# First stage of a hybrid encoder layer: modulation and projection by quarters of K, with four row tiles together

## The chip, the core and the metric

The kernel runs on one core of a Trainium2 chip. The metric is the device time of one execution in microseconds, as the median of several runs. TensorE is called PE here, VectorE DVE, ScalarE ACT, GpSimd POOL and SyncE SP; SP issues the loads and stores of this stage.

## The reference

The input x has 2048 rows of 1024 values (D = 1024), c is one conditioning vector of 1024 values. The reference is one encoder layer; what matters here is its beginning:

```python
mod = silu(c) @ w_mod + b_mod                      # w_mod: 1024 x 6144
shift1, scale1, gate1, shift2, scale2, gate2 = split(mod, 6)
hmix = rms_norm(x, g_norm1) * (1.0 + scale1) + shift1
proj = hmix @ w_in                                 # w_in: 1024 x IN_COLS
q_a, k_a, v_a, q_m, k_m, v_m, o_m, gates = split(proj, ...)
...                                                # windowed attention and a two-way mLSTM,
x = x + gate1 * (concat(att, h_m) @ w_out)         # then the output projection
hff = rms_norm(x, g_norm2) * (1.0 + scale2) + shift2
gte, up = split(hff @ w_ffn_in, 2)
x = x + gate2 * ((silu(gte) * up) @ w_ffn_out)
out = rms_norm(x, g_final)
```

All of it is float32. The modulation is six rows of 1024 values, numbered m = 0 to 5 in the order of the split: m = 1 (scale1) and m = 0 (shift1) are needed before anything can be projected, m = 2 (gate1) and m = 3 to 5 later.

## The kernel before

A product of float32 matrices is made of three products of rounded halves (`mm3`, L56 to L58: high by high, high by low, low by high), so every operand is split into a high part (a rounded copy) and a low part (the difference).

**The first stage** makes, for 16 row tiles of 128 rows (four blocks of four tiles), the "natural" projection: rows on partitions, and 656 columns of w_in: 128 of v_a, 16 of gates and 128 of the first v_m head in one bank (`pa`, 272 columns), the other 384 of v_m in a second one (`pv`). K is 1024, in eight slices k of 128. Its steps:

- *Modulation.* Rows m = 1 and m = 0 are made in halves z of 512 columns. `load_mod` reads a half as four tiles `wmod` of 128 x 2 x 512. `mod_sum` multiplies the slices by the columns of silu(c) (`sc_col`) on DVE and sums them (`macc`, L213 and L215). For two of the four sums, PE takes the first four slices as row products; the row goes through ACT to columns. For the others, four column products with a vector of ones (`modps`, L230) sum over the partitions. `mod_bias` (L237) adds the bias, and `scales` (L328) makes the factor `gs` = (1 + scale) x g.
- *Norm.* For a block of 512 rows: ACT squares and sums (L168), DVE takes the reciprocal root in small steps (`rsqrt`, L106 among them), then the rows are scaled in place (L175 on ACT or L177 on DVE).
- *Transposes.* `turned_split` turns one slice k of a block: PE transposes four 128 x 128 pieces into a bank (`trn`, L183), ACT applies factor and shift (`ntmp`, L184), DVE writes the high part and the low part (`hT`, L190 and L191).
- *Weights.* `load_nat` and `split_nat` load a half of w_in's 656 columns (`wnr`) and split it: ACT writes `wnh` (L346), DVE and POOL share the differences `wnl` (L347).
- *Products.* `nat_mm` (L397) makes the products of one tile over a list of slices k: all k for `pa`, then all k for `pv`.
- *Evictions.* For each tile, ACT writes `vs` from `pa` (L478), DVE its low part and the gates, ACT two pieces of `va`; SP stores `vs` and `va` (L486, L487). `vs` has one buffer.
- *The gate row.* `mod_row(2)` (L359) is drawn, step by step, behind tiles 4, 5 and 6: loads of `wmod` into the buffers big24 to big27, eight sum steps on DVE (`macc`, L375), a split (L141), and two products on PE (`modrow`, L381).

The order on PE is written out by hand (`hand`). On the other engines it is by hand up to `pre.close()` (L439), and a planner orders them behind that. The buffers are reused: x of block 1 lies in big24 to big27, and the weights of modulation in big8 to big15.

Before, tiles 0, 1 and 2 go through k = 0 to 3 when the first half of the modulation is there, and through k = 4 to 7 when the second is. Tile 3 follows in one piece. `EVERY` says behind how many steps of `nat_mm` one slice of the next block is turned; its first row, (0, 0, 0, 2), puts the eight slices of block 1 into tile 3, its second row, eights, two slices of block 2 into each of tiles 4 to 7.

Behind the first stage come the projections in columns, attention, mLSTM, output projection and FFN.

Of the kernel before, what the change touches and what calls it, by code (L numbers as in the profile page):

```python
# [11 lines left out]
F32 = mybir.dt.float32  # L12
# [3 lines left out]
AF = mybir.ActivationFunctionType  # L16
# [20 lines left out]
def hybrid_layer_kernel(  # L37
# [148 lines left out]
    def turned_split(pl, xt, k, gs, shift, dst):  # L186
# [3 lines left out]
        dve.tensor_copy(dst(0, k), t)  # L190
        dve.tensor_tensor(dst(1, k), t, dst(0, k).bitcast(F32), SUB)  # L191

    wm_slots = deque(range(8, 16))

    def load_mod(m, z):

        r = []
        for k in range(0, KT, 2):
            w = big(wm_slots[0], "wmod", (P, 2, 512), F32)
            wm_slots.rotate(-1)  # L200
            sp.dma_start(w, w_mod[k * P:(k + 2) * P, m * D + z * 512:m * D + (z + 1) * 512]
                         .rearrange("(k p) c -> p k c", p=P))
            r.append(w)
        return r

    def mod_sum(pl, m, z, ws_, n_pe):


        acc = pl.tile([P, 512], F32, tag="macc", name="macc")
        for k in range(n_pe, KT):  # L210
            w = ws_[k // 2][:, k % 2, :]
            if k == n_pe:
                dve.tensor_scalar(acc, w, sc_col[:, k:k + 1], None, MUL)  # L213
            else:
                dve.scalar_tensor_tensor(acc, w, sc_col[:, k:k + 1], acc, MUL, ADD)  # L215
        yield True
        if n_pe:
            ps = bank("b", "modrow")
            for k in range(n_pe):
                pe.matmul(ps[:1, :], sc_col[:, k:k + 1], ws_[k // 2][:, k % 2, :], start=k == 0, stop=False)  # L220
            pe.matmul(ps[:1, :], ones[:, 0:1], acc, start=False, stop=True)
            row = pl.tile([1, 512], F32, tag="mrow", name="mrow", bufs=1)
            act.activation(row, ps[:1, :], AF.Copy)
            ps = bank("b", "modps")
            for k in range(4):
                pe.matmul(ps[:, k:k + 1], row[:, k * P:(k + 1) * P], ones[:1, 0:1], start=True, stop=True)
        else:
            ps = bank("d", "modps")
            for k in range(4):
                pe.matmul(ps[:, k:k + 1], acc[:, k * P:(k + 1) * P], ones[:, 0:1], start=True, stop=True)  # L230
        yield True
        mod_bias(m, z, ps)
        yield True

    def mod_bias(m, z, ps):
        o = O_BM + m * KT + 4 * z
        dve.tensor_tensor(mod[:, m, 4 * z:4 * z + 4], ps[:, :4], cols[:, o:o + 4], ADD)  # L237

    wslots = deque()

# [37 lines left out]
    with tc.tile_pool(name="sw", bufs=2, side="right", reuse_waits="tile") as sw:  # L278
# [16 lines left out]
            return r  # L295

        xts = [load_x(0)]
        wm = {(m, 0): load_mod(m, 0) for m in (1, 0)}
# [26 lines left out]
        BD = (slice(0, 4), slice(4, 8))  # L325

        def scales(z):
            dve.scalar_tensor_tensor(gs1[:, BD[z]], mod[:, 1, BD[z]], 1.0, cols[:, O_G1 + 4 * z:O_G1 + 4 * z + 4], ADD, MUL)  # L328

        def load_nat(z):  # L330

            w4 = w_in[z * 512:(z + 1) * 512].rearrange("(k p) c -> p k c", p=P)
            r = [big(16 + 4 * z, "wnr", (P, 4, 144), F32)] + [big(17 + 4 * z + i, "wnr", (P, 2, 512), F32) for i in range(2)]
            sp.dma_start(r[0][:, :, 0:128], w4[:, :, C_VA:C_VA + 128])
            sp.dma_start(r[0][:, :, 128:144], w4[:, :, C_G:C_G + 16])
            for i in range(2):
                sp.dma_start(r[1 + i], w4[:, 2 * i:2 * i + 2, C_VM:C_VM + 512])
            return r

        def split_nat(z, r):  # L340
            ks = BD[z]
            act.activation(wh[:, ks, :144], r[0], AF.Copy)
            dve.tensor_tensor(wl[:, ks, :144], r[0], wh[:, ks, :144].bitcast(F32), SUB)
            for i in range(4):
                k, v = 4 * z + i, r[1 + i // 2][:, i % 2]
                act.activation(wh[:, k, 144:], v, AF.Copy)  # L346
                (pool, dve)[i % 2].tensor_tensor(wl[:, k, 144:], v, wh[:, k, 144:].bitcast(F32), SUB)  # L347

        def norm1(n, xt):
            hT.append(Kt(n, f"hT{n}"))  # L350
# [46 lines left out]
        def nat_mm(n, i, pa, pv, ks):  # L397
            for o, cs in ((pa[:, :NA], slice(0, NA)), (pv[:, :NV], slice(NA, NA + NV))):
                for k in ks:
                    lh, ll = (hT[n](s, k, slice(i * P, (i + 1) * P)) for s in (0, 1))  # L400
                    mm3(o, lh, ll, wh[:, k, cs], wl[:, k, cs], k == 0, k == KT - 1)
                    yield True

        wn = [load_nat(0)]
        wm[1, 1] = load_mod(1, 1)
        wn.append(load_nat(1))
        wm[0, 1] = load_mod(0, 1)
        xts += [load_x(1), load_x(2)]
        for src, o, n in ((g_norm2, O_G2, 8), (conv_b, O_CB, 8), (conv_w[0], O_CW, 24), (g_attn_out, O_GA, 4), (g_mlstm_out, O_GM, 4)):
            sp.dma_start(rows[1][o - N_A:o - N_A + n, :], src.rearrange("o (a b) -> (o a) b", b=P))  # L410
        hT.append(Kt(0, "hT0"))
        ms = {(m, z): mod_sum(s1, m, z, wm[m, z], 4 if m == 1 - z else 0) for z in range(2) for m in (1, 0)}
        ssq = squares(s1, xts[0])
        r = rsqrt(s1, ssq, 4, D, "rs")
        next(ms[1, 0])
        scaled(xts[0], r, True)
        next(ms[0, 0])
        next(ms[1, 0])
        next(ms[1, 0])
        next(ms[0, 0])  # L420
        next(ms[0, 0])
        scales(0)
        split_nat(0, wn[0])
        ops = {i: (bank("gga"[i], "pa"), bank("acc"[i], "pv")) for i in range(3)}
        for k in range(4):
            turned_split(s1, xts[0], k, gs1, mod[:, 0, :], hT[0])
        for i in range(3):
            deque(nat_mm(0, i, *ops[i], range(4)), 0)
        next(ms[1, 1])
        split_nat(1, wn[1])  # L430
        next(ms[1, 1])
        next(ms[1, 1])
        next(ms[0, 1])
        next(ms[0, 1])
        next(ms[0, 1])
        scales(1)
        for k in range(4, KT):
            turned_split(s1, xts[0], k, gs1, mod[:, 0, :], hT[0])
        pre.close()  # L439
        gn = cp.tile([P, 2, 2, HM, NT], F32, name="gn")  # L440
        bgv = bg.rearrange("p (d y h) -> p y d h", d=2, y=2)
        vecs = iter(())
        EVERY = ((0, 0, 0, 2), (8, 8, 8, 8), (2, 0, 0, 0), (0, 0, 0, 0))
        for n in range(NB):
            if n + 1 < NB:
                nrm = norm1(n + 1, xts[n + 1])
                next(nrm)
            if n == 0:
                xts.append(load_x(3))
            if n == 1:  # L450
# [6 lines left out]
                w_first = proj_cols(C_KM)  # L457
            for i in range(4):
                tt = 4 * n + i
                if tt < 3:  # L460
                    pa, pv = ops[i]
                else:
                    pa, pv = bank("g", "pa"), bank("a", "pv")
                ev = EVERY[n][i]
                for j, _ in enumerate(nat_mm(n, i, pa, pv, range(4 if tt < 3 else 0, KT))):
                    if ev and j % ev == ev - 1:
                        next(nrm, None)
# [9 lines left out]
                pav = pa[:, :128].rearrange("p (k d) -> p k d", k=KV)  # L477
                act.activation(vs[:, :, 0, :], pav, AF.Copy)  # L478
                dve.tensor_tensor(vs[:, :, 1, :], pav, vs[:, :, 0, :].bitcast(F32), SUB)
                dve.tensor_tensor(gn[:, :, :, :, tt], pa[:, 128:144].rearrange("p (d y h) -> p y d h", d=2, y=2), bgv, ADD)  # L480
                act.activation(va[:, 0, :128], pa[:, 144:272], AF.Copy)
                act.activation(va[:, 1:, :128], pv[:, :384].rearrange("p (h d) -> p h d", d=128), AF.Copy)
                pool.memset(va[:, :, 128:129], 1.0)
                if tt != 9:
                    next(vecs, None)
                sp.dma_start(vst_d[tt * P:(tt + 1) * P], vs.bitcast(F32))  # L486
                sp.dma_start(vaug_d[tt * P:(tt + 1) * P], va)  # L487
# [1464 lines left out]
```

## Time and profile before

| | |
|---|---|
| runs | 2285.49, 2286.15, 2283.78 us; median 2285.49 |
| span of the profiled execution | 2283.0 us |
| instructions | 32,447 |
| PE busy | 2224.0 us, 97% |
| DVE busy | 1610.1 us, 71% |
| ACT busy | 1058.6 us, 46% |
| POOL busy | 1069.3 us, 47% |
| DMA | 391.28 MB, mean 171 GB/s |

How to read it: the span goes from the first to the last instruction of one profiled execution. The profiled execution's own time is this span, with what lies around it not in the trace; the median of the runs is 2.5 us above it. A row of a trace's timeline has start and duration in us, the engine, the line of the kernel (L), the operation, what it writes and reads, and in brackets the wait ahead of it and what ended it. A row of the groups has busy time in us, mean ns of one, and behind the bar the idle time of the engine just ahead of these instructions with what ended most of it. A row of the windows has the stretch and its length, then the busy us and the instructions (x) of PE, PEld (weight loads), DVE, ACT and POOL, then the granted clock of PE (1.00 is full speed), the busy share of the DMA engines, and GB/s.

### The profile page before, as it was taken

How to read it: one execution, taken by the hardware profiler on the slowest of the kernel's cores; microseconds unless marked ns; L12 is line 12 of the kernel's file. 1: busy time of each engine (PE TensorE's matmuls, PEld its weight loads, DVE VectorE, ACT ScalarE, POOL GpSimd, SP SyncE). 2: the span in 40 equal slices, each digit the busy share in tenths (PEclk: the TensorE clock that was granted, in tenths of full speed). 3: DMA queues.
4: the chain of work that ended last, by engine and by line, in shares of the span. 5: the costliest groups of instructions: out<-in, count | busy, mean ns of one | idle time of the engine just before them, and what ended most of it. 6: DMA issues, size and time to landing. Idle time of an engine off the chain costs nothing.

```text
span 2283.0 us, 32447 instructions
## 1 busy us (share of the span) xinstructions
PE 2224.0 (97%) x10822; PEld 1859.5 (81%) x10822; DVE 1610.1 (71%) x2931; ACT 1058.6 (46%) x2206; POOL 1069.3 (47%) x927
## 2 busy tenths in 40 slices
PE   6999999999999999999999999999999999999998
PEld 4997788888788878788888888788888888888887
DVE  6787577656687887786756776666766666785594
ACT  5433565644577755344444444433333333233352
POOL 1006535334333434536656665566666654592020
PEclk9999999999999999999999999999999999999999
DMA  8476755676666576764353453533333374542462
GB/s 331 157 242 213 238 152 172 186 229 191 194 179 186 177 234 218 267 221 134 111 171 111 152 180 134 178 108 108 100 106 103 105 255 147 162 155 93 140 220 92
DMA packets 352811, 391.28 MB, mean 171 GB/s; under 512 B 21260, under 2 KB 251004, under 8 KB 352644
## 3 DMA queue, kind: packets, MB, share of 16 engines
q1 hardware_dynamic: 352420, 389.18, 52.5%
q8 instruction: 85, 1.39, 0.2%
q14 instruction: 82, 0.67, 0.1%
q10 hardware_dynamic: 224, 0.04, 0.0%
HBM read 269.95 MB, written 119.19 MB: 170 GB/s over the span
## 4 chain that ended last, share of the span: by engine, by line
PE 51%; DVE 3%; DMA 1%; issue 1%; ACT 1%; POOL 1%; SPq 0%; ACTq 0%; POOLq 0%; DVEq 0%
PE fp L56 11%; PE fp L57 11%; PE fp L58 11%; PE fo L58 5%; PE fo L57 5%; PE fo L56 5%; PE ops L56 1%; PE ops L57 1%; DMA al<-a_d 1%; PE ops L58 1%; DVE w L1721 1%; DVE al L1712 1%; DVE ra L1851 1%; PE trn L183 0%; DMA T<-hop_d 0%
## 5 line engine op out<-in xcount | busy, mean ns | idle before, releaser
L498 PE MATMUL gps<-hT,whi 128*128 128x512 f32 x1088 | 397.3, 420 | 0.3 <-DVE cacc L513 0.3
L57 PE MATMUL fo<-w,ah 128*128 128x512 f32 x616 | 239.8, 389 | 1.1 <-DVE w L1721 1.1
L58 PE MATMUL fo<-w,al 128*128 128x512 f32 x616 | 239.8, 389 | 0.5 <-DVE al L1712 0.5
L56 PE MATMUL fo<-w,ah 128*128 128x512 f32 x616 | 239.7, 389 | 0.0
L498 PE MATMUL gps<-hT,wlo 128*128 128x512 f32 x544 | 226.9, 417 | 0.0
L498 PEld LDWEIGHTS gps<-hT,whi 128*128 128x128 f32 x1088 | 200.5, 191 | 24.5 <-DVE cacc L513 0.7
L56 PE MATMUL fp<-T,S 128*128 128x512 f32 x528 | 206.9, 392 | 1.9 <-ACT s L1608 1.9
L57 PE MATMUL fp<-T,S 128*128 128x512 f32 x528 | 205.6, 389 | 0.0
L58 PE MATMUL fp<-T,S 128*128 128x512 f32 x528 | 205.4, 389 | 0.0
L1712 DVE TENSOR_TENSOR al<-al,ah 128x1024 fp32r<-128x1024 f32 x77 | 119.3, 1552 | 109.2 <-ACT ah L1711 109.0
L1711 ACT ACTIVATE ah<-al 128x1024 fp32r<-128x1024 f32 x77 | 81.6, 1060 | 188.5 <-DMA al<-a_d 186.9
L1451 DVE TENSOR_TENSOR S<-sf,S 128x512 fp32r<-128x512 f32 x86 | 130.4, 1554 | 37.4 <-ACT S L1450 37.2
L1451 DVE TENSOR_TENSOR A<-graw,A 128x512 fp32r<-128x512 f32 x86 | 128.4, 1515 | 16.3 <-ACT A L1450 16.3
L58 PE MATMUL fp<-B,A 128*128 128x512 f32 x352 | 136.9, 389 | 0.0
L56 PE MATMUL fp<-B,A 128*128 128x512 f32 x352 | 136.9, 389 | 0.0
L57 PE MATMUL fp<-B,A 128*128 128x512 f32 x352 | 136.9, 389 | 0.0
L57 PEld LDWEIGHTS fo<-w,ah 128*128 128x128 f32 x616 | 115.6, 188 | 25.6 <-DVE w L1721 1.6
L58 PEld LDWEIGHTS fo<-w,al 128*128 128x128 f32 x616 | 115.6, 188 | 24.9 <-DVE al L1712 1.0
L56 PEld LDWEIGHTS fo<-w,ah 128*128 128x128 f32 x616 | 115.6, 188 | 24.3 <-ACT ah L1711 0.2
L1616 DVE SCALAR_TENSOR_TENSOR g<-t,g 128x512 f32<-128x512 f32 x44 | 41.3, 939 | 132.2 <-ACT t L1615 132.2
L1455 POOL TENSOR_TENSOR sf<-A,A22r 128x512 f32<-128x512 f32 x43 | 61.0, 1419 | 154.9 <-DMA A22r<-in_w_ffn_in_dram 130.8
L798 POOL TENSOR_SCALAR ap<-ap,adn 128x384 f32<-128x384 f32 (+1 forms) x128 | 73.0, 590 | 129.2 <-DVE adn L796 71.7
(418 smaller groups left out, 6166.8 us busy)
## 6 DMA issues: line engine op xcount, KB each, us to landing
al<-a_d SPq DMA_DIRECT2D x77, 512.0 KB, 3.8
wmod<-in_w_mod_dram SPq DMA_DIRECT2D x48, 512.0 KB, 7.3
graw<-in_w_ffn_in_dram SPq DMA_DIRECT2D x43, 512.0 KB, 4.0
a_d<-ka SPq DMA_DIRECT2D x66, 256.0 KB, 4.6
bc<-bc_d SPq DMA_DIRECT2D x64, 256.0 KB, 3.7
hop_d<-n SPq DMA_DIRECT2D x56, 256.0 KB, 4.5
a_d<-u SPq DMA_DIRECT2D x55, 256.0 KB, 4.8
mqk<-qk_d SPq DMA_DIRECT2D x44, 256.0 KB, 4.0
```

The source lines that it names most:

```text
L56: pe.matmul(o, lh, rh, start=first, stop=False, skip_group_check=skip)
L57: pe.matmul(o, lh, rl, start=False, stop=False, skip_group_check=skip)
L58: pe.matmul(o, ll, rh, start=False, stop=last, skip_group_check=skip)
L498: pe.matmul(ps, w[i == 2][:, k, :], hT[n](i == 1, k), start=(k == 0 and i == 0), stop=(k == KT - 1 and i == 2))
L798: pool.tensor_scalar(self.p[g][:, :self.NK], self.p[g][:, :self.NK], dn[:, g:g + 1], 0.0, MUL, ADD)
L1451: dve.tensor_tensor(t[:, 1, :], f, t[:, 0, :].bitcast(F32), SUB)
L1455: pool.tensor_tensor(f1, a21, a22, ADD)
L1616: dve.scalar_tensor_tensor(g0, t0, 1.0, g0, ADD, MUL)
L1711: act.activation(ah, al.bitcast(F32), AF.Copy)
L1712: dve.tensor_tensor(al, al.bitcast(F32), ah.bitcast(F32), SUB)
L1721: dve.tensor_tensor(w[:, 1, :], f, w[:, 0, :].bitcast(F32), SUB)
L1851: dve.tensor_tensor(ra[i], ra[i], xr, ADD)
```

## The change

K now goes by quarters q of 256, that is two slices k, and all four tiles of block 0 go through K together.

- *Modulation* (class `Mod`). A quarter of a row m is 256 columns, read as two tiles of 128 x 4 x 256. DVE sums slices in steps of 256 columns. Column products leave the result as columns at once (`product`, two for each slice or sum): in the first quarter PE takes the slices k = 0, 1, 2, 4 and 6 itself, in the other three DVE sums all eight and PE only closes the sum. `close` adds the bias and, for m = 1, makes the quarter of `gs`.
- *Weights* come by quarters: `nat_hi` on ACT, and `nat_lo` wholly on DVE.
- *Transposes of block 0.* `turned_hi`: ACT reads the bank twice, and writes the high part and `ntmp`; DVE only subtracts.
- *Products.* `few_mm(i, k)` makes the products of tile i with one slice k. Four tiles have six banks: two of tag g, shared by two tiles each, and four of tags a and c; an odd tile has 240 columns in the shared bank and 416 in its own. `outs` says where the evictions find the columns.
- *Order.* The main loop over q places loads, sums, transposes and products. Loads of x for blocks 1 and 2 stand in the third quarter. Behind `pre.close()`, tile 0's turn makes the last products of k = 6 and 7 for tiles 0 and 1, tiles 2 and 3 follow; tiles 4 and 5 then run as a pair, two slices k at a time, with the slices of block 1 turned just ahead of them (`nrm1`). `EVERY` becomes ((0,0,0,0), (0,0,4,4), ...): block 2's slices go into tiles 6 and 7.

Behind tile 8 the instructions of every engine stand in the same order in both kernels. The diff, cut to its core:

```diff
+    def turned_hi(pl, ps, k, gs, shift, dst):
+        act.activation(dst(0, k), ps, AF.Identity, bias=shift[:, k:k + 1], scale=gs[:, k:k + 1])
+        t = pl.tile([P, 512], F32, tag="ntmp", name="ntmp", bufs=2)
+        act.activation(t, ps, AF.Identity, bias=shift[:, k:k + 1], scale=gs[:, k:k + 1])
+        dve.tensor_tensor(dst(1, k), t, dst(0, k).bitcast(F32), SUB)
...
-    def load_mod(m, z):
...
-    def mod_sum(pl, m, z, ws_, n_pe):
...
+    class Mod:
+        def __init__(self, m, q, on_pe):
...
+                w = big(wm_slots[0], "wmod", (P, 4, 256), F32)
+                wm_slots.rotate(-1)
+                sp.dma_start(w, w_mod[k * P:(k + 4) * P, m * D + q * 256:m * D + (q + 1) * 256]
+                             .rearrange("(k p) c -> p k c", p=P))
+        def part(self, pl, h):
+            for k in range(4 * h, 4 * h + 4):
+                w = self.w[h][:, k % 4, :]
+                if k in self.on_pe:
+                    continue
+                if self.acc is None:
+                    self.acc = pl.tile([P, 256], F32, tag="macc", name="macc", bufs=3)
+                    dve.tensor_scalar(self.acc, w, sc_col[:, k:k + 1], None, MUL)
+                else:
+                    dve.scalar_tensor_tensor(self.acc, w, sc_col[:, k:k + 1], self.acc, MUL, ADD)
+        def product(self, w, col, tag, last=False):
+            for j in range(2):
...
+                pe.matmul(self.ps[:, j:j + 1], w[:, j * P:(j + 1) * P], col, start=first, stop=last, skip_group_check=True)
...
+        def close(self, tag):
+            self.product(self.acc, ones[:, 0:1], tag, True)
+            m, o = self.m, O_BM + self.m * KT + 2 * self.q
+            qs = slice(2 * self.q, 2 * self.q + 2)
+            dve.tensor_tensor(mod[:, m, qs], self.ps[:, :2], cols[:, o:o + 2], ADD)
+            if m:
+                dve.scalar_tensor_tensor(gs1[:, qs], mod[:, 1, qs], 1.0, cols[:, O_G1 + 2 * self.q:O_G1 + 2 * self.q + 2], ADD, MUL)
...
+        def load_quarter(q):
+            wm[1, q] = Mod(1, q, () if q else (0, 1, 2, 4, 6))
+            wn[q] = load_nat(q)
+            wm[0, q] = Mod(0, q, () if q else (0, 1, 2, 4, 6))
...
-        def split_nat(z, r):
...
-                (pool, dve)[i % 2].tensor_tensor(wl[:, k, 144:], v, wh[:, k, 144:].bitcast(F32), SUB)
+        def nat_lo(q, i):
+            k, r = 2 * q + i, wn[q]
+            dve.tensor_tensor(wl[:, k, 144:], r[1][:, i], wh[:, k, 144:].bitcast(F32), SUB)
...
+        def few_mm(i, k):
+            two = ((spare[i // 2][:, 272 * (i % 2):(512 if i % 2 else 272)], slice(0, (272, 240)[i % 2])),
+                   (ops[i][:, :(384, 416)[i % 2]], slice((272, 240)[i % 2], NA + NV)))
...
+        for q in range(4):
+            if q < 2:
+                load_quarter(q + 2)
+            if q == 2:
+                xts.append(load_x(1))
...
+                xts.append(load_x(2))
+            k = 2 * q
+            turned_hi(s1, trn[k], k, gs1, mod[:, 0, :], hT[0])
+            nat_hi(q, 1)
+            nat_lo(q, 1)
+            turned_hi(s1, trn[k + 1], k + 1, gs1, mod[:, 0, :], hT[0])
+            if q == 3:
+                break
+            for i in range(4):
+                few_mm(i, k)
+            wm[1, q + 1].part(s1, 0)
+            wm[1, q + 1].part(s1, 1)
+            wm[1, q + 1].close("b")
+            nat_hi(q + 1, 0)
+            nat_lo(q + 1, 0)
+            for i in range(2):
+                few_mm(i, k + 1)
+            trn[k + 2] = turns(xts[0], k + 2, "b")
+            wm[0, q + 1].part(s1, 0)
+            wm[0, q + 1].part(s1, 1)
+            wm[0, q + 1].close("d")
+            for i in range(2, 4):
+                few_mm(i, k + 1)
+            trn[k + 3] = turns(xts[0], k + 3, "d")
         pre.close()
...
-        EVERY = ((0, 0, 0, 2), (8, 8, 8, 8), (2, 0, 0, 0), (0, 0, 0, 0))
+        EVERY = ((0, 0, 0, 0), (0, 0, 4, 4), (2, 0, 0, 0), (0, 0, 0, 0))
...
+                if tt < 4:
+                    for j in (((6, 0), (6, 1), (7, 0), (7, 1)), (), ((6, 2), (7, 2)), ((6, 3), (7, 3)))[i]:
+                        few_mm(j[1], j[0])
+                    pg, vm = outs(i)
+                elif tt == 4:
+                    two = [(bank("g", "pa"), bank("a", "pv")) for _ in range(2)]
+                    next(nrm1)
+                    for k in range(0, KT, 2):
+                        for j in range(2):
+                            next(nrm1, None)
+                            deque(nat_mm(n, j, *two[j], (k, k + 1)), 0)
...
```

More of the change, by code (lines that the diff above doesn't have):

```diff
@@ L191, in turned_split @@
         dve.tensor_tensor(dst(1, k), t, dst(0, k).bitcast(F32), SUB)
-    wm_slots = deque(range(8, 16))
-    def load_mod(m, z):
[L197 to L204, printed above, removed]
-    def mod_sum(pl, m, z, ws_, n_pe):
[L209 to L233, printed above, removed]
@@ L416, in hybrid_layer_kernel @@
[L416 to L430, printed above, removed]
@@ L431, in hybrid_layer_kernel @@
[L431 to L438, printed above, removed]
+        for i in range(4):
+            if i % 2:
+                act.activation(xts[0][i], xts[0][i], AF.Copy, scale=r[:, i:i + 1])
+            else:
+                dve.tensor_scalar(xts[0][i], xts[0][i], r[:, i:i + 1], None, MUL)
+        wm[1, 0].products(0, "c")
```

121 lines of the change are left out of this document (78 added, 43 removed).

## The prediction

> **What bounds the kernel now.** I read the page first, then the windows of the first 80 us, since the change ends there.
>
> ```profile
> span 2283.0 us, 32447 instructions
> PE   6999999999999999999999999999999999999998
> ```
>
> Behind the first slice PE is at 9 tenths almost to the end, and the order of instructions on every engine behind the first stage is the same in both kernels. So the change is worth what it moves the point at which PE gets into its steady run.
>
> ```profile
> 20.00:30.00 10.00, 6.44 (x30) 5.63 (x30) 7.90 (x15) 4.88 (x8) 2.52 (x2) 0.66 1.09 388
> 30.00:40.00 10.00, 9.37 (x57) 8.41 (x58) 9.68 (x13) 3.98 (x7) 3.25 (x3) 1.00 1.05 409
> 40.00:50.00 10.00, 9.07 (x45) 5.27 (x44) 5.28 (x11) 2.78 (x5) 0.00 (x0) 1.00 0.79 319
> 50.00:60.00 10.00, 8.72 (x42) 7.20 (x41) 8.39 (x26) 8.88 (x17) 0.00 (x0) 0.83 0.60 224
> 70.00:80.00 10.00, 8.76 (x62) 8.18 (x61) 9.20 (x32) 7.51 (x17) 0.21 (x2) 1.00 0.59 155
> ```
>
> The columns are PE, PEld, DVE, ACT, POOL, clock, DMA share, GB/s. DMA is full to 40 us, and DVE is busy for 17.6 of the 20 us ahead of that: the modulation sums feed the columns that PE waits for. In the last row PE runs without them; it meets one more wait ahead of tile 4. My yardstick is the transpose with which tile 8 begins:
>
> ```profile
> 63.18 0.29 PE L56 MATMUL pa<-wnh,hT 128*128 128x272 f32 x1
> 64.68 0.33 PE L56 MATMUL pv<-wnh,hT 128*128 128x384 f32 x1
> 66.79 0.29 PE L56 MATMUL pa<-wnh,hT 128*128 128x272 f32 x1
> ...
> 77.17 0.60 PE L183 MATMUL trn<-ident,xt 128*128 128x128 f32 x4
> 79.01 0.26 PE L310 MATMUL colps<-ident,rows 48*128 48x48 f32 x1 [1.25 <-ACT ntmp L184]
> ...
> 95.43 0.48 PE L381 MATMUL modrow<-macch,ones_r 128*128 128x512 f32 x1
> ...
> 112.41 0.60 PE L183 MATMUL trn<-ident,xt 128*128 128x128 f32 x4
> 112.76 0.37 PE L56 MATMUL pa<-wnh,hT 128*128 128x272 f32 x1
> ```
>
> Before: tiles 0 to 3 and the eight transposed columns of block 1 are done with the row at 77.17, so by about 77.5; tile 4 begins behind the row at 79.01, tile 8 at 112.4. Twelve pa and twelve pv products take 66.79 - 63.18 = 3.61, so one group of the new few_mm (one tile, one k, the same 656 columns three times) takes 0.90. A transposed column costs PE 112.76 - 112.41 = 0.35.
>
> **Part by part: the quarters on DVE.** The sums now run in steps of 256 columns, 54 of them instead of 24 of 512; the row products on PE go, POOL's share of the wnl subtractions comes to DVE, and the cast of hT goes to ACT, which reads the bank twice.
>
> ```profile
> L215 DVE SCALAR_TENSOR_TENSOR macc<-wmod,sc_col,macc 128x512 f32<-128x512 f32 x20 | 16.9, 843 | 0.8
> L191 DVE TENSOR_TENSOR hT<-ntmp,hT 128x512 fp32r<-128x512 f32 x8 | 5.5, 692 | 0.3
> L177 DVE TENSOR_SCALAR xt<-xt,rsy 128x1024 f32<-128x1024 f32 x4 | 2.7, 749 | 0.0
> L347 DVE TENSOR_TENSOR wnl<-wnr,wnh 128x512 fp32r<-128x512 f32 x4 | 2.6, 683 | 0.0
> L213 DVE TENSOR_SCALAR macc<-wmod,sc_col 128x512 f32<-128x512 f32 x4 | 1.9, 481 | 0.7 <-DMA wmod<-in_w_mod_dram 0.7
> L106 DVE SCALAR_TENSOR_TENSOR rsy<-rsa,rsy 128x4 f32<-128x4 f32 x6 | 1.0, 162 | 0.2
> L237 DVE TENSOR_TENSOR mod<-modps,cols 128x4 f32<-128x4 f32 x4 | 0.6, 160 | 6.0 <-PE modps L226 3.2 <-PE modps L230 2.9
> ...
> L681 DVE SCALAR_TENSOR_TENSOR sc<-sps,ng 128x256 f32<-128x256 f32 x64 | 26.6, 415 | 7.7 <-PE ktp L612 4.4 <-PE sps L679 1.4 <-ACT cacc L528 1.2
> L1087 DVE SCALAR_TENSOR_TENSOR ma<-ma,cols,arb 128x256 f32<-128x256 f32 x32 | 13.2, 475 | 6.1 <-PE arb L1083 6.1
> ```
>
> A step of 256 is not in the old stage; L681 and L1087 bound it at 0.415 and 0.475. I take 0.475, since it too adds onto its own operand, and 0.03 for the hand-over between dependent steps. The first step (a plain scaling) I put at 0.35, between 0.481 and 0.162. A sum of eight is then 0.35 + 7 x 0.505 = 3.9. [...]
>
> ```profile
> 13.65 0.16 DVE L106 SCALAR_TENSOR_TENSOR rsy<-rsa,rsy 128x4 f32<-128x4 f32 x1
> 25.34 1.16 DVE L328 SCALAR_TENSOR_TENSOR gs<-mod,cols 128x4 f32<-128x4 f32 x1
> ...
> 42.23 0.95 PE L230 MATMUL modps<-ones_r,macc 128*128 128x1 f32 x8
> ...
> L168 ACT ACTIVATE junk<-xt 128x1024 bf16<-128x1024 f32 x8 | 8.4, 1051 | 7.3 <-DMA xt<-in_x_dram 7.3
> L184 ACT ACTIVATE ntmp<-trn,mod,gs 128x512 f32<-128x512 f32 x8 | 6.0, 775 | 3.8 <-DVE hT L191 1.8 <-PE trn L183 1.0 <-DVE gs L328 0.9
> L346 ACT ACTIVATE wnh<-wnr 128x512 fp32r<-128x512 f32 x8 | 4.6, 623 | 0.7 <-DMA wnr<-in_w_in_dram 0.5
> ```
>
> First quarter: the root ends at 13.8; one sum step ahead of it 0.35, two scalings 1.5, the two sums' rest 0.35 + 4 x 0.5, two closes, wnl 0.7 + 0.4, three small ones 0.5: its modulation stands at about 21 (before: 26.5 for the first half). A close is two column products (0.95 / 4 each) with hand-overs, 0.6, and DVE waits behind it, as L237's row shows.
>
> Each later quarter is one chain, for DVE takes its work in order. Both columns' lower halves come ahead of the next sums: ACT's two passes 1.55, its wnh split 0.62, two passes 1.55, the subtraction 0.69, 4.4 together with DVE idle for half of it. Then sum 3.9, close 0.6, bias and scale 0.35, wnl 1.1, sum 3.9, close 0.6, bias 0.2: 15.0. PE needs 8 x 0.90 + 2 x 0.35 + 1 = 9, so DVE sets the pace: modulation at 36, 51 and 66. In the last quarter DVE's order puts the norms of blocks 1 and 2 in between: 25 small steps of 0.18 and eight scalings of 0.70, 10 us which before lay under PE's run behind the second half. So the last two lower halves, due at 66 + 4.4, come at 79.5. Five to six groups follow: tile 3 ends at 85, against 77.5 minus the 2.8 of transposes that it held.
>
> The loads are ahead of this: 13 MB at 400 GB/s are in by 40 us. [...]
>
> **Tile 4's start.** Block 1's transposes moved from inside tile 3 to the pair of tiles 4 and 5, and on ACT all eight L184 stand behind the evictions of tiles 0 to 3. These go through one vs buffer, so each waits until the store of the last has landed.
>
> ```profile
> 78.26 0.32 SPq L486 DMA_DIRECT2D vst_d<-vs  x1
> ...
> DMA to landing us min/median/max: 1.7/5.6/6.0
> ...
> 83.44 0.28 ACT L478 ACTIVATE vs<-pa 128x128 fp32r<-128x128 f32 x1 [4.21 <-DMA vst_d<-vs]
> ```
>
> A round is vs 0.28, its lower half 0.3, issue 0.3 and landing: 2.6 at the shortest landing, 5.5 as in the row. Before, the four rounds were spread from 56 to 78 us; now they all begin at 82, when tile 0's last group is done. The queue is nearly free then, so I take 3.4: the fourth vs at 92, its copies 1.0, then L184 and the cast 1.2: tile 4 begins at 94.6. Behind that waiting vs on ACT stands all that feeds PE.
>
> **Tiles 4 to 8.** 32 groups 28.9, 14 transposed columns 4.9, two row sums 1.2: 35.0. In the pair, the second column of each two is transposed right ahead of its use; transpose, L184, cast and subtraction take 2.3 and the first products cover 0.4 and part of the third: 1.2 each in three places, 3.6. Then the gate row: its loads reuse block 1's buffers, free after the last transpose of the pair; before, two whole tiles lay between these and L381 at 95.43, now 3.6 us of products.
>
> ```profile
> L375 DVE SCALAR_TENSOR_TENSOR macc<-wmod,sc_col,macc 128x512 f32<-128x512 f32 x56 | 42.5, 759 | 2.3 <-DMA wmod<-in_w_mod_dram 1.2
> ...
> DMA to landing us min/median/max: 4.0/7.3/10.1
> ...
> 92.77 0.63 ACT L141 ACTIVATE macch<-macc 128x512 fp32r<-128x512 f32 x1 [1.84 <-DVE macc L375]
> ```
>
> Landing 4.0, eight steps 6.0, ACT 0.6, DVE 0.7 are 11.3; less 3.6 and the stall of 1.2 in it, PE waits 6.5, and about 1 more at the second row.
>
> ```profile
> 577.00:579.00 2.00, 0.00 (x0) 0.00 (x0) 1.19 (x8) 0.00 (x0) 0.42 (x1) 0.90 0.50 113
> 579.00:581.00 2.00, 1.33 (x5) 1.25 (x6) 0.56 (x1) 0.00 (x0) 1.33 (x3) 0.50 1.13 354
> ```
>
> Here PE starts again after a standstill, and the clock is 0.50; two such, at tile 4 and at the gate row, cost 1.7 each. Sum: 94.6 + 35.0 + 3.6 + 7.5 + 3.4 = 144, against 112.4: 31.7 later, and I take off 0.7 for waits of PE behind tile 8 that then shrink: +31 on the profiled 2283.0, or on the median of 2285.5, which is 2.5 above it: **2316**. Low ends (steps at 0.415, rounds of 2.6, no slow clock) make +20, high ends (rounds of 5, slow clock longer) +42.
>
> **Rivals.** *Only DVE's pace counts* (0.15): evictions and gate row find cover; tile 4 at 88, tile 8 at 127, so 2300. For it: the 1.7 of landing. Against: the order on ACT. *The clock stays down* (0.15): PE works 60% of the time in this stage, and between 50 and 60 us it fell to 0.83 with PE busy for 8.7 of 10; the last groups and the pair's first half at 1.8 instead of 0.90 make some +7 more: 2323. [...] *Faster* (0.10): DVE's chain overlaps so far that PE sets the pace, 9 us a quarter. Then tile 3 ends at 60 and, if the stores land in time, tile 4 begins at 63 and tile 8 at 107: 2281. For it: PE's idle start and its 10 us of modulation at 42 to 52. It decides below some 10 us a quarter with the norms hidden; I find 15. *Absorbed later* (0.03): 2285.5. My case has 0.57.
>
> **Numbers.** Own case 2305 to 2327; with 2300 and 2323 in, and a little below, the range is 2298 to 2328. A measurement here tells 0.2% (4.6 us) from no change: faster 0.10, same 0.03, slower 0.87.
>
> **What would show it.** Right: the mod additions some 15 us apart, the last L198 near 80, DVE's idle time there charged to ACT's ntmp and PE's modps; ACT's vs waiting for vst_d three times and PE idle some 9 us ahead of tile 4; 6 us on macch. Wrong, if quarters come every 10 us, or tile 8 begins before 125.

## The result, and the profile after

The changed kernel takes 2324.5 us (median of five runs, 2321.6 to 2326.41) against 2285.49 for the kernel before; the ratio is 1.017, with a 95% interval of 1.016 to 1.0181. The profiled execution has a span of 2324.3, against 2283.0: 41.3 us more. 2316 was forecast, with 2298 to 2328.

PE's row of slices from the page, then from the timelines of the changed kernel the modulation sums of m = 0 on DVE and the transpose that ends tile 7 (the yardstick of the prediction). Three slices at the start are low now, where it was one:

```profile
PE   6689999999999999999999999999999999999998
...
24.27 0.16 DVE L249 TENSOR_TENSOR mod<-modps,cols 128x2 f32<-128x2 f32 x1 [4.21 <-PE modps L238]
39.46 0.16 DVE L249 TENSOR_TENSOR mod<-modps,cols 128x2 f32<-128x2 f32 x1 [1.05 <-PE modps L238]
57.10 0.16 DVE L249 TENSOR_TENSOR mod<-modps,cols 128x2 f32<-128x2 f32 x1 [1.17 <-PE modps L238]
76.90 0.16 DVE L249 TENSOR_TENSOR mod<-modps,cols 128x2 f32<-128x2 f32 x1 [0.81 <-PE modps L238]
...
153.63 0.60 PE L183 MATMUL trn<-ident,xt 128*128 128x128 f32 x4
```

Tile 7 ends at 153.63 in place of 112.41, 41.2 us later, and that is the whole difference of the spans: the rest takes 2170.7 after and 2170.6 before. The later quarters, from one modulation sum to the next, take 15.2, 17.6 and 19.8 us. Behind them, on PE, ACT and DVE:

```profile
94.96 0.57 PE L56 MATMUL pa<-wnh,hT 128*128 128x240 f32 x1 [8.00 <-ACT va L553]
101.42 0.36 PE L56 MATMUL pa<-wnh,hT 128*128 128x272 f32 x1 [0.86 <-DVE hT L190]
110.20 0.39 PE L56 MATMUL pa<-wnh,hT 128*128 128x272 f32 x1 [1.01 <-DVE hT L190]
110.93 0.39 PE L58 MATMUL pa<-wnh,hT 128*128 128x272 f32 x1 [0.21 <-DVE hT L191]
132.63 0.80 PE L401 MATMUL modrow<-macch,ones_r 128*128 128x512 f32 x1 [6.00 <-ACT macch L141]
...
92.73 0.28 ACT L548 ACTIVATE vs<-pa 128x128 fp32r<-128x128 f32 x1 [1.01 <-DMA vst_d<-vs]
94.63 0.28 ACT L553 ACTIVATE va<-pa 128x128 f32<-128x128 f32 x1 [1.62 <-DVE gn L550]
100.04 1.45 ACT L184 ACTIVATE ntmp<-trn,mod,gs 128x512 f32<-128x512 f32 x2 [0.55 <-PE trn L183]
...
92.89 1.42 DVE L177 TENSOR_SCALAR xt<-xt,rsy 128x1024 f32<-128x1024 f32 x2
94.22 0.28 DVE L549 TENSOR_TENSOR vs<-pa,vs 128x128 fp32r<-128x128 f32 x1
```

The first row is new: tile 3's last products wait 8.00 us. They write columns 272 to 511 of a bank whose first 272 columns are tile 2's, and the wait ends with tile 2's eviction (the second ACT row). That eviction waits 1.01 us for the store of tile 1's vs, and 1.62 for DVE, where two scalings of block 3 stand ahead of the lower half of vs (the two DVE rows). The second row is tile 4's first product, 22.2 us later than in the kernel before (its row below); from there to the end of tile 7 go another 19.0. The next two rows are one of three like waits in the pair, the last is the gate row's. From PE's timeline of the kernel before:

```profile
79.20 0.39 PE L56 MATMUL pa<-wnh,hT 128*128 128x272 f32 x1
```

The clock of the changed kernel in three stretches of the quarters (the column behind POOL is the granted clock):

```profile
40.00:44.00 4.00, 4.00 (x17) 3.84 (x16) 1.29 (x2) 1.77 (x4) 0.00 (x0) 0.50 1.01 339
56.00:60.00 4.00, 3.92 (x15) 3.93 (x16) 1.38 (x3) 2.70 (x4) 0.00 (x0) 0.50 0.38 146
68.00:72.00 4.00, 3.64 (x19) 3.08 (x18) 3.66 (x13) 1.52 (x4) 0.00 (x0) 0.68 0.00 0
```

### The profile page after: what moved, and what is told of

Its sections match the earlier page's. It is cut to its first block, busy times and chain, and to the rows that moved or that the text cites. A ratio compares the mean times of both kernels' runs of the same rounds, so it can differ in the third digit from the quotient of the medians.

```text
span 2324.3 us, 32530 instructions
## 1 busy us (share of the span) xinstructions
PE 2237.8 (96%) x10842; PEld 1879.2 (81%) x10842; DVE 1627.9 (70%) x2967; ACT 1062.2 (46%) x2214; POOL 1061.1 (46%) x923
## 4 chain that ended last, share of the span: by engine, by line
PE 53%; DMA 1%; DVE 1%; issue 1%; ACT 1%; POOL 1%; SPq 0%; POOLq 0%; ACTq 0%; DVEq 0%
PE fp L56 11%; PE fp L57 11%; PE fp L58 11%; PE fo L58 6%; PE fo L57 6%; PE fo L56 6%; PE ops L56 1%; PE ops L58 1%; PE ops L57 1%; DMA B<-hop_d 0%; PE trn L183 0%; DMA T<-hop_d 0%; DMA al<-a_d 0%; DVE S L1524 0%; DMA A22r<-in_w_ffn_in_dram 0%
## 5 line engine op out<-in xcount | busy, mean ns | idle before, releaser
L1524 DVE TENSOR_TENSOR A<-graw,A 128x512 fp32r<-128x512 f32 x86 | 133.3, 1574 | 11.1 <-ACT A L1523 11.1
```

The source lines that it names most:

```text
L1524: dve.tensor_tensor(t[:, 1, :], f, t[:, 0, :].bitcast(F32), SUB)
```

## The experiments

All start from the changed kernel. In all of them the order of instructions differs from it in the first stage alone. What lies behind the end of tile 7 took 2168.6 to 2178.0 us in these traces, so a single time says less than the end of tile 7; where the differences come from was found for e10 alone, and only in part. Beside these runs the kernel before had medians of 2285.94 to 2287.84; the changed kernel was not run again beside them. The traces differ a little too: the kernels of e1, e3 and e5 are the changed one up to their edits, yet their last modulation sum comes anywhere from 75.31 to 77.06. So differences of some 2 us, in the time or at the end of tile 7, are not told apart here.

In the table, the last column is the end of tile 7 less that of the changed kernel:

| | median, us | span | end of tile 7 | against after |
|---|---|---|---|---|
| before | 2285.49 | 2283.0 | 112.41 | -41.2 |
| after | 2324.50 | 2324.3 | 153.63 | |
| e1, three vs buffers | 2323.52 | 2323.2 | 149.82 | -3.8 |
| e2, tile 3 ahead of the eviction | 2318.49 | 2315.3 | 146.71 | -6.9 |
| e3, gate row a tile later | 2317.52 | 2317.5 | 142.34 | -11.3 |
| e4, scalings on ACT | 2321.89 | 2319.1 | 146.70 | -6.9 |
| e5, columns further ahead | 2317.72 | 2316.3 | 141.87 | -11.8 |
| e6, three slices on PE | 2320.04 | 2317.3 | 143.37 | -10.3 |
| e7, second column earlier | 2322.65 | 2321.8 | 147.39 | -6.2 |
| e8, all seven | 2298.70 | 2295.9 | 123.09 | -30.5 |
| e9, balanced | 2294.82 | 2296.6 | 121.20 | -32.4 |
| e10, ACT by hand | 2299.13 | 2294.9 | 117.23 | -36.4 |
| e11, PE kept busy | 2324.47 | 2323.9 | 151.37 | -2.3 |
| e12, e10 with PE kept busy | 2299.13 | 2296.6 | 118.57 | -35.1 |

**e1: three vs buffers.**

```diff
-                vs = sw.tile([P, KV, 2, HD], F32R, tag="vs", name="vs", bufs=1)
-                va = sw.tile([P, HM, 129], F32, tag="va", name="va")
+                vs = sw.tile([P, KV, 2, HD], F32R, tag="vs", name="vs", bufs=3)
+                va = sw.tile([P, HM, 129], F32, tag="va", name="va", bufs=2)
```

The second pair of lines names the two buffers that va has from its pool in any case.

> vs gets three buffers instead of one. Theory (the evictions of tiles 0 to 3 run one store at a time, and PE's wait of 8.00 us ahead of tile 3's last products and the start of tile 4 both hang on that): vs of tiles 0, 1 and 2 follow each other, tile 2's bank is read by about 89.5 in place of 94.9, the wait of 8.00 shrinks to about 3, tile 4's first product comes at about 96 in place of 101.4: 2319. Rival (the squares of block 3, which stand between the evictions on ACT, hold them, the stores do not): under 2 us, 2323.

From the timelines of ACT and PE:

```profile
87.09 0.27 ACT L548 ACTIVATE vs<-pa 128x128 fp32r<-128x128 f32 x1
89.04 0.27 ACT L548 ACTIVATE vs<-pa 128x128 fp32r<-128x128 f32 x1
89.64 0.30 ACT L548 ACTIVATE vs<-pa 128x128 fp32r<-128x128 f32 x1
91.84 0.57 PE L56 MATMUL pa<-wnh,hT 128*128 128x240 f32 x1 [4.33 <-ACT va L553]
98.15 0.37 PE L56 MATMUL pa<-wnh,hT 128*128 128x272 f32 x1 [0.97 <-DVE hT L190]
```

The stores' part is there: the third vs comes 3.1 us earlier, PE's wait falls from 8.00 to 4.33, tile 4 begins 3.3 earlier. That is some three fifths of what I expected. Squares of block 3 (L168, 1.06 each) still stand between the evictions, as the rival had it, and the time is the rival's 2323. So the truth lies between the two: the stores were a part of the wait, not the whole.

**e2: tile 3's last products ahead of tile 2's eviction.**

```diff
-                    for j in (((6, 0), (6, 1), (7, 0), (7, 1)), (), ((6, 2), (7, 2)), ((6, 3), (7, 3)))[i]:
+                    for j in (((6, 0), (6, 1), (7, 0), (7, 1)), (), ((6, 2), (7, 2), (6, 3), (7, 3)), ())[i]:
```

> Tile 3's last products stand on PE ahead of tile 2's eviction, not behind it, so that they need not wait for the bank that the two tiles share. Theory (the stores set the pace, the shared bank only shows it): the wait of 8.00 us goes at its place and PE waits ahead of tile 4 and 5 instead; 1 to 3 us earlier, 2322.5. Rival (the shared bank is a loss of its own): 8 us and the slow clock behind it, 2315.

```profile
90.59 0.77 ACT L184 ACTIVATE ntmp<-trn,mod,gs 128x512 f32<-128x512 f32 x1
91.64 0.28 ACT L548 ACTIVATE vs<-pa 128x128 fp32r<-128x128 f32 x1 [0.28 <-DMA vst_d<-vs]
95.35 0.28 ACT L548 ACTIVATE vs<-pa 128x128 fp32r<-128x128 f32 x1 [0.93 <-DMA vst_d<-vs]
94.11 0.57 PE L56 MATMUL pa<-wnh,hT 128*128 128x272 f32 x1 [1.73 <-DVE hT L190]
```

Tile 4 begins 7.3 us earlier, though the stores still follow each other on one buffer: the expectation failed and its rival held, though the time, 2318.5, lies between the two. With tile 3 done early, block 1's transposes come early, and the planner puts the first L184 ahead of the vs that waits for a store. e1 shortened the evictions and left the tie through the shared bank, and tile 4 gained 3.3; e2 left the evictions and took the tie away, and tile 4 gained 7.3. So the wait of 8.00 was the chain of evictions as PE met it through the shared bank, which held PE and, through PE, block 1's transposes. The edit also changed ACT's order; what the tie and what that order gave are not parted.

**e3: the gate row one tile later.**

```diff
-                if tt != 9:
+                if tt not in (5, 9):
                     next(vecs, None)
```

> The gate row's first two products stand behind tile 6 in place of behind the pair, the second two behind tile 7. Theory: PE's wait of 6.00 us for macch goes, with 1.5 us of slow clock behind it: 2317. Rival (the clock has no part): 2318.5. Rival (the wait turns up again, since the eviction of tile 5 and the columns of block 2 are late too): within 2 us of 2324.5.

The wait for macch is gone, and tile 7 ends 11.3 us earlier. Of this, 2.1 came ahead of tile 4 already (its first product at 99.28), where the kernels do not differ, and 0.5 is the second pair of row products, which now stands behind tile 7. Some 8.7 remain: the wait of 6.00, and about 2.5 for products behind it, which ran at half pace from 132.6 to 137.4 in the changed kernel, with the clock at 0.50. In e3 the same products behind the row (from 133.80 us) take 0.29 each and come 0.12 to 0.13 apart, for 0.43 and 0.23 in the changed kernel. The time, 2317.5, is the theory's, but with runs from 2315.2 to 2320.6 it cannot rule out the 2318.5 of the rival without the clock; these times can.

**e4: the scalings of blocks 1 and 2 on ACT.**

```diff
-            scaled(xt, rsqrt(s1, squares(s1, xt), 4, D, "rs"))
+            scaled(xt, rsqrt(s1, squares(s1, xt), 4, D, "rs"), n < 3)
```

> The eight scalings of blocks 1 and 2 run on ACT, not on DVE. By the prediction's term (the norms lie wholly on the path, eight scalings of 0.70): 5.6 us earlier, 2319. By the trace of after (four scalings of 0.75 stand ahead of the last modulation sum's end, the others cost 0.6): 3.5 us earlier, 2321, if ACT takes them in its idle 7.5 us ahead of the last quarter. Rival (they stand in front of ACT's own passes of the last quarter): no gain or up to 2 us later, 2325.

```profile
74.57 0.16 DVE L249 TENSOR_TENSOR mod<-modps,cols 128x2 f32<-128x2 f32 x1 [0.49 <-PE modps L238]
79.15 0.69 DVE L198 TENSOR_TENSOR hT<-ntmp,hT 128x512 fp32r<-128x512 f32 x1 [1.60 <-ACT ntmp L197]
```

The last sum comes 2.3 us earlier, the last lower half 3.4 (79.15 for 82.59): the reading of the trace, not the prediction's whole-path term, and the time (2321.9) agrees. Tile 7 gains more, 6.9: tile 4 begins 4.4 earlier, the products of 384 columns in the pair come 0.17 to 0.18 apart from 98.9 us on, where the changed kernel has 0.32 at 103.8 to 104.8 and a clock of 0.50 from 104 to 106, and the gate row waits 4.99 in place of 6.00.

**e5: two more columns turned ahead of the pair.**

```diff
-                    next(nrm1)
+                    for _ in range(3):
+                        next(nrm1)
                     for k in range(0, KT, 2):
```

> Two more columns of block 1 are turned ahead of the pair of tiles 4 and 5, so that each column is turned four groups of products ahead of its use in place of two. Theory (the three waits of 1.0 and 0.2 us in the pair are the chain transpose, pass, cast, subtraction): they go; 3 to 3.5 us earlier, tile 8 at about 150 in place of 153.6, 2321. Rival (PE is held up at the pair's start for as much, since the banks b and d must be read first): within 1 us of 2324.5.

The windows of after and then of e5 at the same place, and e5's gate row:

```profile
104.00:106.00 2.00, 2.00 (x10) 1.91 (x9) 0.00 (x0) 0.00 (x0) 0.00 (x0) 0.50 0.00 0
106.00:108.00 2.00, 2.00 (x12) 2.00 (x12) 0.92 (x2) 0.78 (x1) 0.00 (x0) 0.76 0.04 8
```

```profile
104.00:106.00 2.00, 2.00 (x16) 1.96 (x16) 1.12 (x2) 0.54 (x2) 0.00 (x0) 1.00 0.00 0
106.00:108.00 2.00, 2.00 (x16) 1.97 (x16) 1.12 (x2) 0.54 (x2) 0.00 (x0) 1.00 0.00 0
121.06 0.49 PE L401 MATMUL modrow<-macch,ones_r 128*128 128x512 f32 x1 [3.75 <-ACT macch L141]
```

More than three times the expectation. Tile 4 begins 1.1 earlier, the waits in the pair go (3.6), the clock stays at 1.00 in it, and block 1's x is free earlier, so that the gate row's loads start earlier and PE waits 3.75 in place of 6.00.

**e6: three slices on PE in quarters 2 to 4.**

```diff
-            wm[1, q] = Mod(1, q, () if q else (0, 1, 2, 4, 6))
+            wm[1, q] = Mod(1, q, (0, 2, 4) if q else (0, 1, 2, 4, 6))
...
+            for h in range(2):
+                wm[1, q + 1].products(h, "b")
             wm[1, q + 1].close("b")
```

(and the same for m = 0).

> In quarters 2 to 4 PE takes the slices 0, 2 and 4 of both sums as column products, and DVE sums five slices in place of eight: DVE has 3.1 us less in a quarter, PE 2.8 more. Theory (DVE's sums pace the quarter where PE waits for macc: 3.09, 1.81, 3.08, 2.10 and 4.24 us in after): each of these waits shrinks by 1.55 and is filled with 1.4 of products: 4 to 5 us earlier over the three quarters, 2320. Rival (the slow clock of PE in this stage comes from these waits, and goes with them): 9 us, 2315. Rival (PE's own order sets the pace): no gain, 2324.

```profile
24.30 0.16 DVE L249 TENSOR_TENSOR mod<-modps,cols 128x2 f32<-128x2 f32 x1 [4.22 <-PE modps L238]
66.39 0.16 DVE L249 TENSOR_TENSOR mod<-modps,cols 128x2 f32<-128x2 f32 x1 [0.47 <-PE modps L238]
```

The three quarters take 42.1 us in place of 52.6: 10.5 less, the size of the rival with the clock. What the clock gave of it was not taken apart: over the whole run it reads 0.991 for 0.987, and DVE still waits 2.42 and 2.43 us for the second column in the third and fourth quarters (2.90 and 2.89 in the changed kernel). The time, 2320.0 with runs from 2314.6 to 2326.3, cannot tell the two apart.

**e7: the second column ahead of two groups.**

```diff
-            for i in range(2, 4):
-                few_mm(i, k + 1)
             trn[k + 3] = turns(xts[0], k + 3, "d")
+            for i in range(2, 4):
+                few_mm(i, k + 1)
```

> The second column of the next quarter is turned ahead of the last two groups of products, not behind them. Theory (DVE waits 2.9 us in each of quarters 2 to 4 for the lower half of this column, since its transpose stands on PE behind two groups at a slow clock; the prediction had the transposes ready): about 2 us a quarter, 6 us earlier, 2318.5. Rival (the two groups then come later by as much and hold the next sum's end): within 1 us of 2324.5.

The last lower half comes at 76.70, 5.9 us earlier, and tile 7 ends 6.2 earlier. The trace has the expected 6; of the time only 2 (2322.65) shows.

**e8: all seven.**

> All seven edits together. Theory (the terms stand one behind the other, so they add up): by the first four runs' start of tile 8, evictions and bank 8, gate row 8, norms 5, and by the expectations of the other three 3.5, 4.5 and 6: 35 us earlier, tile 8 at about 119, 2290. Rival (one wait's loss lies in another's shadow): 20 us or less, 2304.

The single gains add up to 57 us at the end of tile 7, together they are 30.5, and the time is 2298.7, between theory and rival. Each gain above holds some of another's slow clock or wait. From PE's timeline, and ACT's:

```profile
81.02 1.12 PE L183 MATMUL trn<-ident,xt 128*128 128x128 f32 x4 [3.34 <-DVE cols L342]
85.60 1.97 PE L183 MATMUL trn<-ident,xt 128*128 128x128 f32 x8 [3.46 <-ACT ntmp L184]
...
83.69 1.18 ACT L175 ACTIVATE xt<-xt,rsy 128x1024 f32<-128x1024 f32 x1
84.73 1.48 ACT L184 ACTIVATE ntmp<-trn,mod,gs 128x512 f32<-128x512 f32 x2
```

PE ends tile 3 at about 76.8 and then waits: ACT, which was idle, now has the scalings (moved there) and the squares of block 3 ahead of block 1's passes.

**e9 and e10: balanced, and ACT's order by hand.** e9: PE takes two slices in quarters 2 to 4, only block 1's scalings run on ACT, block 3's load and the small columns come later. e10: also ACT's order by hand up to tile 5, with x of block 1 loaded a quarter earlier and two columns of block 1 turned behind tile 3's products.

> The seven edits together, better balanced: PE takes two slices in quarters 2 to 4 (three of eight for m = 0 in the first), only block 1's scalings run on ACT, x of block 3 and the small columns come later in the program. In the run with all seven, ACT's eight scalings and the squares of block 3 stood ahead of block 1's passes, PE was idle for most of 77 to 86, and a quarter took 14.0 us with PE busy throughout. Theory: tile 4 begins some 7 us earlier, the quarters give 3 to 5 more: tile 8 at 113 to 115, 2287. Rival (the planner still puts the squares of block 3 ahead of the evictions on ACT): 5 us of it stay away, 2292.

> As the last, with ACT's order by hand up to tile 5: norm of block 1 in the gaps of quarters 2 and 3, squares of block 2 in the third, of block 3 behind the pair; two columns of block 1 are turned behind tile 3's products and passed ahead of the evictions of tiles 2 and 3. Theory: nothing but PE's own work and DVE's sums is left on the path; modulation at 22.6, 35, 47.5 and 60, tile 3 done at 71, tile 4 at 73, tile 8 at 108 to 110: 2282, faster than both. Rival (the slow clock of PE stays, a quarter takes 14 us as in the run with all seven): tile 8 at 114, 2287, no faster than the kernel before.

Both theories failed. A quarter stays at 15, 14 and 14 us in both, as e10's rival had it, and the slow clock still comes once in each quarter (in e10's windows of 4 us, 0.67 from 36, 0.70 from 52 and 0.58 from 64 us). But both end later than their rivals: e9 at 2294.8 for 2292 (ratio to before 1.0037, 1.0023 to 1.0051), e10 with tile 7 at 117.2 for 114 and at 2299 for 2287. e10 ends tile 7 4 us earlier than e9, but gives this back before the first stage is over: the first product behind that stage comes 76.9 us after tile 7 in place of 70.3. It waits at tile 8 for block 3's scalings on DVE, some 3 us; the rest was not traced.

**e11: PE kept busy in the quarters.** `close` first makes 6 or 12 products that nobody reads:

```diff
         def close(self, tag):
+            if self.q:
+                warm = bank(tag, "modps")
+                for _ in range(6 if self.m else 12):
+                    pe.matmul(warm[:, 128:512], ones_r, wh[:, 0, :384], start=True, stop=True, skip_group_check=True)
             self.product(self.acc, ones[:, 0:1], tag, True)
```

> As the changed kernel, with products added that nothing reads: ahead of the close of each sum in quarters 2 to 4 PE multiplies ones with a part of wnh into unused columns of the same bank, 6 products of 384 columns ahead of m = 1 and 12 ahead of m = 0 (0.175 each at full clock: 1.05 and 2.1 us), in the time in which it waits for macc (1.81 to 4.24 us). Theory (the clock of 0.50 in 38 to 46, 56 to 62 and 69 to 79 comes from these standstills, and costs DVE 1.7 us a quarter through the column that is turned behind two slow groups): the granted clock stays near 1.00 there, tile 8 at 148 to 150 in place of 153.6, 2320. Rival (the clock falls for another reason, or DVE's sums alone set the pace): tile 8 within 1 us of 153.6 or later by what the products hold up, 2325.

```profile
40.00:44.00 4.00, 3.90 (x27) 3.79 (x28) 1.46 (x3) 2.91 (x5) 0.00 (x0) 1.00 0.90 284
56.00:60.00 4.00, 4.00 (x29) 3.86 (x28) 2.12 (x9) 3.89 (x7) 0.00 (x0) 1.00 0.97 359
68.00:72.00 4.00, 4.00 (x16) 3.88 (x16) 3.26 (x14) 0.00 (x0) 0.00 (x0) 0.50 0.00 0
```

That the standstills bring the slow clock is shown, in one trace: the first two windows, at 0.50 in after, are at 1.00. What it is worth is less than I had it: the third quarter is 2.4 us shorter (15.2), but the second is 1.4 longer, held by the added products, and in the last the planner put block 1's scalings ahead of the first sum's end, PE waited 4.70 us, and the clock fell again (third window). Tile 7 ends 2.3 earlier; the time is unchanged.

**e12: e10 with PE kept busy**, by 14 products of 128 columns ahead of the first group of quarters 2 and 3, and with block 3's squares inside the pair.

> As the run with ACT's order by hand, with two edits: 14 products of 128 columns that nothing reads fill PE's wait of 1.6 us between the close of m = 0 and the first products of quarters 2 and 3, and the squares of block 3 stand on ACT inside the pair, so that its scalings come before tile 8's end. Theory (this wait, behind the thin column products, still sets the clock to 0.50 for some 4 us in each quarter, which is why a quarter takes 14 us): a quarter takes 12.5, tile 8 comes at about 115 in place of 119.6, and 2.8 us of waits at tile 8 go: 2290, still no faster than the kernel before. Rival (the clock falls all the same): tile 8 at 119, 2295.

Rows of e12:

```profile
36.81 0.16 DVE L249 TENSOR_TENSOR mod<-modps,cols 128x2 f32<-128x2 f32 x1 [0.70 <-PE modps L238]
50.82 0.16 DVE L249 TENSOR_TENSOR mod<-modps,cols 128x2 f32<-128x2 f32 x1 [0.70 <-PE modps L238]
39.32 1.68 PE L486 MATMUL pv<-wnh,ones_r 128*128 128x128 f32 x14
```

The place that I meant to fill, in e10:

```profile
36.63 0.61 PE L238 MATMUL modps<-ones_r,macc 128*128 128x1 f32 x4 [1.16 <-DVE macc L231]
37.49 1.11 PE L204 MATMUL trn<-ident,xt 128*128 128x128 f32 x4 [0.25 <-DVE mod L249]
38.26 0.57 PE L56 MATMUL pa<-wnh,hT 128*128 128x272 f32 x1
```

The theory's clock came: it reads 1.00 in every window from 24 to 64. But from sum to sum the quarters take 14.1, 14.0 and 16.0, where e10 has 14.8, 14.0 and 14.1; the added products stand in the last two, and in the last DVE also waits 1.85 us for block 2's squares on ACT. In e10 the 1.6 us lie between the close's start and the first wide product behind it, 36.63 to 38.26; the added products stand two groups later, right ahead of the next four, and hold these by 1.5 us (39.32 to 40.83). So they took about what the clock could have given: without them a quarter would be some 12.5, an estimate that no run here has tried. Nor is it shown that they kept the clock up: in e10 it falls at about 37.3 and 51.0 (worked out from 0.67 in the window from 36 to 40 and 0.87 in that from 48 to 52), ahead of their places. What the clock is worth in the 14 us stays open. No version here beats the kernel before.

## Why the prediction was right, and where its terms were off

The sign and the place held: the whole loss lies in the first stage, behind a chain through DVE, ACT and PE that sets a quarter's pace. The size, 2324.5, lies in the forecast range, but above its middle: 41.2 us at the end of tile 7 against 31.7 forecast. That it is not further off is in part luck, for terms that were too small and one that was too large offset each other. Of the signs, the sums came 15 to 20 us apart in place of 15, the last L198 at 82.6 (near 80), and 6.00 on macch as forecast; of three waits of vs for its store one came (1.01 us); and PE's 9 idle us ahead of tile 4 came in size, 8.00 and 0.86, but most of them inside tile 3, for the shared bank. Going by the steps:

- *First quarter*, forecast 21, measured 24.27. The term that failed is PE's own: I counted DVE's steps and priced a column product at 0.95 / 4 = 0.24. PE makes ten of them for five slices, each two records in the trace, and they took 0.44 each. e9 and e10, in which PE takes three slices of m = 0 in place of five, have this sum at 22.45 and 22.52.

```profile
11.70 4.40 PE L238 MATMUL modps<-sc_col,wmod 128*128 128x1 f32 x20 [5.82 <-DMA wmod<-in_w_mod_dram]
```

- *A sum of eight*, 0.35 + 3.54 forecast. The seven steps took 3.61, 0.516 each, so my 0.505 from the nearest row was right.

```profile
28.79 3.61 DVE L231 SCALAR_TENSOR_TENSOR macc<-wmod,sc_col,macc 128x256 f32<-128x256 f32 x7
```

- *A later quarter*, forecast 15.0. The second quarter took 15.2, the third 17.6. There I had missed a link: the second column's transpose stands on PE behind two groups (its row below), which take 1.73 each (39.29 to 42.75, clock 0.50 from 40 on) where I counted 0.90, and DVE waits for it. e7 took it away.

```profile
42.75 1.05 PE L204 MATMUL trn<-ident,xt 128*128 128x128 f32 x4
45.32 0.69 DVE L198 TENSOR_TENSOR hT<-ntmp,hT 128x512 fp32r<-128x512 f32 x1 [2.90 <-ACT ntmp L197]
```

- *Norms of blocks 1 and 2*, forecast 10 on the path. By the trace the small steps slip between the dependent sum steps at next to no cost (the sum steps start 0.51 to 0.55 apart with one or two between, 0.516 without) and only scalings count (1.06 apart with one of 0.75 between); e4 gives 2.3 to 3.4 for them. This oversized term made up for much of what the terms ahead of it were short of: the last lower half came at 82.59 to 83.3, forecast 79.5.
- *Tile 4's start*, forecast 94.6, measured 101.42. Of the 6.8, 3.5 come from the step above. The eviction chain was there, but not as I had it. The vst stores landed in 3.0 at the median, near the 2.5 that my round of 3.4 holds; the squares and scalings of block 3, 1.06 and 0.7 each, which stand in that chain on ACT and DVE and wait there for x, I had put at nothing; and PE met the chain inside tile 3, through the shared bank, as e2 shows. That wait of 8.00 was in no step of the prediction. Nor were tile 3's last products, which run at half pace behind it, 1.8 us more at a clock of 0.50. How much block 3's norms alone cost was not tried. The 8.00 us stand ahead of products into other columns of that bank than the ones ACT reads (va, L553); why these wait for each other was not shown, and I had not reckoned with it.
- *The pair*, 3.6 of waits forecast; measured 3 x (1.0 + 0.21) = 3.6. *The gate row*, 6.5 forecast and 6.00 measured; the second row's wait of 1 did not come.
- *Slow clock*, 3.4 forecast behind tile 4's start, as two restarts of 1.7 each. No row of the kernel before shows this 1.7; the window that I took it from shows the clock of 0.50 alone. From tile 4's first product to the end of tile 7 the trace has 52.2; 35.0 of work, 3.6 and 6.0 leave 7.6. Of these, 4.2 are products at half pace while the clock reads 0.50: 1.7 from 103.5 to 106.9, 2.5 from 132.6 to 137.4. The other 3.4 were not taken apart. So the time came out near the 2323 of the rival with the clock that stays down, but not by its mechanism alone: the clock reads 1.00 again from 107 to 130 us, it cost 1.8 in tile 3 and 1.7 in the pair where the rival had some 7, and 6.8 of the 9.5 us by which tile 7 is later than forecast lie ahead of tile 4.
- *What brings the slow clock.* e11 shows it for waits of PE: with products in them (3.09 and 3.08 us of idle time became 1.00 and 0.96), the windows from 40 to 44 and 56 to 60 us read 1.00 in place of 0.50. In the changed kernel it fell at about 38.7 and 55.8 us, around the end of the waits of 3.09 and 3.08 us, not behind the one of 1.81, and at 69.4, 1.7 us behind the one of 2.10 in the last quarter; the 4.24 of that quarter came when it was down already. How long a wait has to be was not shown. With transposes ahead of the wait of 3.09 and the thin products of the close behind it, PE has no wide product from 35.2 to 39.3, 4.1 us; whether that is what counts was not tried. In the pair the clock fell behind a wait of only 0.86 us, at about 103.6 us, some 3 us after it had come back; in e5, with a wait of 0.43 there, it reads 1.00 from 98 to 118 us.

The rivals *faster* and *absorbed later* are out: in no run did a later quarter take less than 13.5 us, and what the changed kernel lost in the first stage was not given back.

## What to carry to other kernels

When a stage is cut into finer steps so that work can start sooner, add up the chain through all engines for one step, transposes and closes included: here a step of 15 us on a chain of DVE, PE and ACT replaced a PE run that had needed them only twice. Before two tiles share a PSUM bank (here one that holds products of both, such as `pa`), look for an eviction of the one that stands ahead of products of the other, which here waited 8.00 us for it. And gains of single edits need not add up: here seven that gave 57 us one by one gave 30 together, for each held some of another's wait.

## What the runs showed of the hardware

Early in the stage of the changed kernel the granted clock does not tell PE's pace. In its windows from 24 to 28 and 28 to 32 it reads 1.00, yet the same product takes half again as long there (0.52) as four groups later (0.33), and steps of 0.32 from one to the next became 0.17:

```profile
27.40 0.52 PE L57 MATMUL pv<-wnl,hT 128*128 128x384 f32 x1
27.72 0.52 PE L58 MATMUL pv<-wnh,hT 128*128 128x384 f32 x1
33.62 0.33 PE L57 MATMUL pv<-wnl,hT 128*128 128x384 f32 x1
33.79 0.34 PE L58 MATMUL pv<-wnh,hT 128*128 128x384 f32 x1
```

The column products of 0.44 in the first quarter against 0.24 later (0.95 for four in e12) fit the same half pace. Behind some 12 us of products of one column and transposes (11.7 to 24.2 us) the products of 384 columns came 0.32 apart, and behind 6 us of wide ones (25.3 to 31.8) 0.17. Why the clock record differs there was not tried.
